# The last two down slabs of a feed-forward stage taken together by output block, and two more buffers for weight halves

## The chip, the cores and the metric

One core of a Trainium2 chip runs the whole kernel. The metric is the time of one execution on the device in microseconds (us); lower is better. Matmuls run on TensorE (PE), vector work on VectorE (DVE), activations and casts on ScalarE (ACT), a few sums on GpSimd (POOL). Transfers are issued from the queues of SyncE (SP) and of ACT.

## The reference, cut to what matters

The input passes through a first block (two layers) and a second block (four layers). A layer of the second block is a mixer (`swa`, `gla`, `fox`, `swa` in turn) and a feed-forward stage, each behind a norm with a learned shift and scale:

```
for i in range(4):
    mod = silu(c) @ ada_w[i] + ada_b[i]
    sh1, sc1, g1, sh2, sc2, g2 = split(mod, 6)
    h = rmsnorm_2(x, norm_gain[i, 0]) * (1 + sc1) + sh1
    x = x + g1 * mixer_i(h)                       # swa, gla, fox, swa
    h = rmsnorm_2(x, norm_gain[i, 1]) * (1 + sc2) + sh2
    g, u = split(h @ w_gu[i], 2)
    x = x + g2 * ((silu(g) * u) @ w_down[i])      # feed-forward
return rmsnorm_2(x, final_norm)
```

There are 256 tokens, 1024 channels and 22 x 128 hidden channels in the feed-forward stage. Everything is float32.

## The kernel before

**Split products.** Each float32 operand is split into a rounded half and the rest (`wh` and `wl` for weights, `gH` and `gL` or `fh` and `fl` for activations), and a product is three matmuls: `wh` by `xH`, `wl` by `xH`, `wh` by `xL` (mm3, L251). In `u_unit` (L397) the same is done for data that isn't normalised yet.

**Weight slabs.** `load_slab` fetches 1 MB of weights into `raw` (three buffers, SP queue) and splits it in two tiles of 1024 columns: ACT casts (`wh`, L161) and DVE subtracts (`wl`, L162). There are four buffers each for `wh` and `wl` (`WB`), so two slabs. In swa layers a tile is split by one instruction, in the other stages by two.

**The feed-forward stage** (`layer2b`) runs over eleven pairs of hidden chunks s = 0 to 10. For each it makes two gate/up units (48 matmuls into a `pm` bank), then silu, a product, and the split into `fh` and `fl`; then the down slab of the pair before (`kacc`) adds 48 matmuls into four accumulator banks `acc`, each of which holds two of the eight output blocks. The last down slab runs by itself: after each bank `x_update` (L969) adds the two finished blocks to the state `xT` on DVE. Per block it also makes the next layer's unnormalised input (`u_feed`: ACT gH L367, DVE gL L368) and the squares for the norm (ACT `sq`, POOL `ssum`).

**Between two stages** the next stage starts with units on the unnormalised input, 48 matmuls each (one in swa layers, two in gla and fox and before each feed-forward stage). In the midst of them come the matmuls that sum the squares (`ms`, L331), and what is left of the units behind the last `ms` covers the chain: ACT `rstd` (Ln L288, Exp L290), then for each of eight channel tiles k a DVE `hn` (L428), an ACT `gH` (L435) and a DVE `gL` (L436). The first unit on normalised data needs tile 0, then 1, and so on.

**The join of the two blocks** is such a place with a double norm (`jn`, `jt`, `jr`: L1016 to L1021; gH L1028, gL L1029). Block 2 opens a pool `cm` with its constants (`band`, `rcos`, `rsin`, `gwa`, `gwg`, `tri`, `causal`, `wf`, `bf`: ten loads from ACT's queue, L896), and the pools of a layer (`zp`, `work`) follow behind `cm` in memory. A pool that reuses memory waits for its last readers. `mi` (L1223) is a first tile of a layer's pool.

**Order.** Each engine works through its instructions in the order that a scheduler fixed when the kernel was built. The numbers `F_AT` and `PADS` shift where tiles lie in memory.

Of the kernel before, what the change touches and what calls it, by code (L numbers as in the profile page):

```python
# [11 lines left out]
F32R = mybir.dt.float32r  # L12
# [41 lines left out]
SCRATCH = 1024  # L54
ROW = 320
SIDE = 32
F_AT = (4, 12, 24)
PADS = (40, 8, 80)
WB = 4
PERM = np.concatenate([np.arange(0, T, 2), np.arange(1, T, 2)])  # L60

# [38 lines left out]
class Kern:  # L100
    def __init__(self, ctx, tc, a):
        self.ctx, self.tc, self.nc, self.a = ctx, tc, tc.nc, a
        nc = self.nc
        self.const = ctx.enter_context(tc.tile_pool(name="const", bufs=1))
        self.slab = ctx.enter_context(tc.tile_pool(name="slab", bufs=1))
        self.act = ctx.enter_context(tc.tile_pool(name="act", bufs=1))
        self.hp = ctx.enter_context(tc.tile_pool(name="hp", bufs=2))
        self.psms = ctx.enter_context(tc.tile_pool(name="psms", bufs=1, space=PSUM))
        self.psum = ctx.enter_context(tc.tile_pool(name="psum", bufs=1, space=PSUM))
        self.ffn, self.nmain = False, 0  # L110
        self.ada = self.ada_stream()
        self.cact = None
        self.rate, self.credit = 0.0, 0.0
        self.ada_done = 0
        self.modc = {}
        self.ms = None
        self.u = None
        self.gates = []
        self.splits = SPLITS
        self.slab_ins = [None] * 8  # L120
        self.fin = None
        self.nuid = 0
        self.load_consts()
        self.const.tile([128, PADS[0]], F32, tag="pad", name="pad0")
        self.hp.tile([128, PADS[1]], F32, tag="pad", name="pad1", bufs=1)

# [38 lines left out]
    def load_slab(self, dram):  # L165
# [12 lines left out]
                next(self.ada, None)  # L178
        return parts

    def split_slab(self, raw):
        parts = []
        for i in range(2):
            H = self.slab.tile([128, 1024], F32R, tag="wh", name=self.uid("wh"), bufs=WB)
            L = self.slab.tile([128, 1024], F32R, tag="wl", name=self.uid("wl"), bufs=WB)
            for q in range(self.splits):
                n = 1024 // self.splits
                c = slice(q * n, (q + 1) * n)
                ins = self.split(raw[:, i * 1024 + q * n:i * 1024 + (q + 1) * n], H[:, c], L[:, c])
                self.slab_ins[i * self.splits + q] = ins  # L190
            parts.append((H, L))
        return parts
# [697 lines left out]
    def block2(self):  # L890
        nc, tc, a = self.nc, self.tc, self.a
        with ExitStack() as ctx:
# [15 lines left out]
            self.fox_bf = cload("bf", [16, 1], a["fox_bf"][0])  # L908
            self.tri = cload("tri", [128, 2, T], a["tri"])
            self.cm.tile([128, PADS[2]], F32, tag="pad", name="pad2")  # L910
            for i in range(DEPTH_2):
                for half in range(2):
                    self.nsq, self.ffn = 3 if (i, half) == (1, 0) else NSQ, half == 1
                    with ExitStack() as lctx:
                        self.zp = lctx.enter_context(tc.tile_pool(name=f"z2_{i}_{half}", bufs=1))
                        self.work = lctx.enter_context(tc.tile_pool(name=f"wk2_{i}_{half}", bufs=2))
                        (self.layer2a if half == 0 else self.layer2b)(i)
# [31 lines left out]
    def acc_banks(self, n=4):  # L949
        return [self.ps("a", "acc") for _ in range(n)]  # L950

    def kacc(self, banks, dram, xs, first, last, after=None):
        parts = self.load_slab(dram)
        for n in range(8):
            for i, (xH, xL) in enumerate(xs):
                H, L = parts[i]
                self.mm3(banks[n // 2][:, (n % 2) * 256:(n % 2) * 256 + 256],
                         H[:, n * 128:(n + 1) * 128], L[:, n * 128:(n + 1) * 128], xH, xL,
                         first and i == 0 and n % 2 == 0, last and i == 1)
            if after and n % 2 == 1:  # L960
                after(n - 1)
                after(n)

    def x_update(self, n, ps, g):
        xv = self.xT[:, n, :]
# [96 lines left out]
    def layer2b(self, i):  # L1062
        nc, a = self.nc, self.a
# [6 lines left out]
        banks = None  # L1070
        pend = []
        nslab = NFF // 2
# [1 line left out]
        def upd(n):  # L1074
            self.x_update(n, banks[n // 2][:, (n % 2) * 256:(n % 2) * 256 + 256], m[:, 40:48])

        def down(s):
            self.kacc(banks, a["w_down"][i, s], pend[s], s == 0, s == nslab - 1,
                      upd if s == nslab - 1 else None)

        for s in range(nslab):
            self.rate = R_FFN if S_ADA <= s < nslab - 1 else 0.0
            xs = []
            for jj in (2 * s, 2 * s + 1):
                t = self.work.tile([128, T], F32, tag="ft", name=self.uid("ft"), bufs=2)
# [8 lines left out]
                else:  # L1094
                    ps = self.unit(a["w_gu"][i, jj], h, "T")
                    last = nc.scalar.activation(t, ps[:, 0:256], AF.Silu)
                    nc.vector.tensor_mul(t, t, ps[:, 256:512])
                f0 = F_AT[s % len(F_AT)]
                H, L = [self.work.tile([128, T + 64], F32R, tag=n, name=self.uid(n), bufs=6)[:, f0:f0 + T]
                        for n in ("fh", "fl")]  # L1100
                self.split(t, H, L)
                xs.append((H, L))
            pend.append(xs)
            if s >= 1:
                if s == 1:
                    banks = self.acc_banks()
                down(s - 1)
            if s == nslab - 1:
                self.preload_ln(last)
        if i + 1 == DEPTH_2:  # L1110
# [1 line left out]
        else:  # L1112
            self.prep_layer(i + 1)
            self.u_begin(self.gp[:, 0:8], self.modc[i + 1][:, 0:8])
        down(nslab - 1)
        if i + 1 == DEPTH_2:
            self.final()

# [524 lines left out]
```

## Time and profile before

| | |
|---|---|
| time, median of 3 runs | 2106.68 us (2104.94 to 2107.19) |
| the profiled execution: its time, its span | 2103.22 us, 2101.3 us |
| PE busy / DVE busy / ACT busy | 2070.5 / 1627.9 / 1203.9 us |
| weight loads by TensorE busy (beside the matmuls) | 2016.7 us |
| mean granted clock of TensorE | 0.998 |
| bytes read by the core | 448 MB, 214 GB/s |

The span is what the trace covers; the time of the run holds 1.92 us more. PE is busy for all but 30.8 us of the span.

### The profile page before, as it was taken

The numbers are of one execution on the slowest core, as the hardware profiler recorded it, in microseconds if no ns is written. First come the engines' busy times: TensorE is split into PE (matmuls) and PEld (weight loads), VectorE is DVE, ScalarE is ACT, GpSimd is POOL, SyncE is SP. The second block draws the span as 40 slices with busy tenths as digits, with TensorE's granted clock in tenths as the row PEclk, the third lists the DMA queues.
The fourth block names the chain that finished last, engine by engine and source line by source line (L and its number), as shares of the span: only waits on it lengthen the run. The fifth ranks groups of instructions, "written<-read, shape, count | busy, mean of one in ns | idle before, by whom it ended". The sixth has DMA issues, their size and how long they took to land.

```text
span 2101.3 us, 42506 instructions
## 1 busy us (share of the span) xinstructions
PE 2070.5 (99%) x17176; PEld 2016.7 (96%) x17176; DVE 1627.9 (77%) x3347; ACT 1203.9 (57%) x2533; POOL 70.7 (3%) x89
## 2 busy tenths in 40 slices
PE   8999999999999999989999999999999999999998
PEld 7999999999999999978999999999989999879998
DVE  7877678997777788797877787877776878868554
ACT  7665555566655554666444666544656544566444
POOL 0000010010000000111000000000000000001000
PEclk9999999999999999999999999999999999999999
DMA  7557668865576578732887432888443888424542
GB/s 265 181 170 257 211 220 292 305 246 191 169 251 221 191 272 316 248 127 90 294 300 279 161 141 101 289 294 284 177 161 121 287 294 309 163 81 170 192 181 101
DMA packets 87830, 452.02 MB, mean 215 GB/s; under 512 B 9978, under 2 KB 19393, under 8 KB 46546
## 3 DMA queue, kind: packets, MB, share of 16 engines
q1 hardware_dynamic: 74736, 438.34, 58.5%
q10 hardware_dynamic: 12898, 10.97, 2.2%
q8 instruction: 134, 2.20, 0.4%
q14 instruction: 62, 0.51, 0.1%
HBM read 448.17 MB, written 1.11 MB: 214 GB/s over the span
## 4 chain that ended last, share of the span: by engine, by line
PE 94%; DVE 4%; ACT 2%; issue 1%; DMA 0%; POOL 0%; DVEq 0%; ACTq 0%
PE pm L251 67%; PE acc L251 11%; PE pa L397 4%; PE pa L251 2%; DVE wl L162 1%; PE po L251 1%; PE ms L331 1%; PE pa L574 1%; PE pa L1134 1%; PE po L1158 1%; ACT s L1143 1%; PE pa L1392 1%; PE pt L1155 0%; PE po L670 0%; PE pa L640 0%
## 5 line engine op out<-in xcount | busy, mean ns | idle before, releaser
L162 DVE TENSOR_TENSOR wl<-raw,wh 128x512 fp32r<-128x512 f32 (+1 forms) x1240 | 832.4, 705 | 276.4 <-ACT wh L161 271.9
L161 ACT CAST wh<-raw 128x512 fp32r<-128x512 f32 (+1 forms) x1240 | 719.2, 632 | 418.3 <-PE pm L251 207.3
L251 PE MATMUL pm<-gH,wh 128*128 128x256 f32 x2112 | 591.4, 281 | 2.1 <-ACT gH L161 2.1
L251 PE MATMUL pm<-gH,wl 128*128 128x256 f32 x2112 | 591.7, 281 | 0.1
L251 PE MATMUL pm<-gL,wh 128*128 128x256 f32 x2112 | 589.6, 281 | 0.1
L251 PEld LDWEIGHTS pm<-gH,wh 128*128 128x128 f32 x2112 | 397.1, 188 | 4.5 <-ACT gH L161 2.8
L251 PEld LDWEIGHTS pm<-gH,wl 128*128 128x128 f32 x2112 | 396.9, 188 | 3.3 <-issue 2.1
L251 PEld LDWEIGHTS pm<-gL,wh 128*128 128x128 f32 x2112 | 395.9, 188 | 3.4 <-issue 2.4
L251 PE MATMUL pm<-hH,wh 128*128 128x256 f32 x1328 | 374.2, 282 | 1.0 <-DVE mrg L162 0.7
L251 PE MATMUL pm<-hL,wh 128*128 128x256 f32 x1328 | 372.8, 281 | 0.8 <-DVE hL L162 0.8
L251 PE MATMUL pm<-hH,wl 128*128 128x256 f32 x1328 | 372.3, 280 | 0.0
L205 DVE CUSTOM_DVE_ANT_0 araw<-araw,cact,pv 128x1024 f32<-128x1024 f32 x192 | 244.3, 1281 | 20.1 <-DMA araw<-ada 19.8
L251 PEld LDWEIGHTS pm<-hH,wh 128*128 128x128 f32 x1328 | 249.7, 188 | 3.6 <-ACT hH L161 1.4
L251 PEld LDWEIGHTS pm<-hL,wh 128*128 128x128 f32 x1328 | 249.7, 188 | 1.4 <-DVE hL L162 1.2
L251 PEld LDWEIGHTS pm<-hH,wl 128*128 128x128 f32 x1328 | 249.7, 188 | 0.5
L251 PE MATMUL acc<-fh,wl 128*128 128x256 f32 x704 | 196.0, 281 | 0.0
L251 PE MATMUL acc<-fh,wh 128*128 128x256 f32 x704 | 194.2, 280 | 0.0
L251 PE MATMUL acc<-fl,wh 128*128 128x256 f32 x704 | 192.5, 281 | 0.0
L251 PEld LDWEIGHTS acc<-fh,wl 128*128 128x128 f32 x704 | 132.2, 188 | 0.0
L251 PEld LDWEIGHTS acc<-fh,wh 128*128 128x128 f32 x704 | 131.6, 188 | 0.0
L251 PEld LDWEIGHTS acc<-fl,wh 128*128 128x128 f32 x704 | 130.4, 188 | 0.0
L251 PE MATMUL pm<-wh,gH 128*128 128x256 f32 x352 | 100.0, 286 | 6.0 <-DVE rt L1175 2.7
(356 smaller groups left out, 3246.1 us busy)
## 6 DMA issues: line engine op xcount, KB each, us to landing
raw<-w_in SPq DMA_DIRECT2D x104, 1024.0 KB, 5.0
araw<-ada SPq DMA_DIRECT2D x192, 512.0 KB, 4.7
raw<-w_gu SPq DMA_DIRECT2D x88, 1024.0 KB, 5.6
raw<-w_down SPq DMA_DIRECT2D x44, 1024.0 KB, 6.1
raw<-swa_w SPq DMA_DIRECT2D x12, 1024.0 KB, 4.7
raw<-gla_w SPq DMA_DIRECT2D x12, 1024.0 KB, 5.4
raw<-fox_w SPq DMA_DIRECT2D x12, 1024.0 KB, 4.8
raw<-w_mem_kv SPq DMA_DIRECT2D x8, 1024.0 KB, 4.8
```

Of the source, the lines that this page charges most:

```text
L161: i1 = self.nc.scalar.copy(H, src)
L162: i2 = self.nc.vector.tensor_sub(L, src, H.bitcast(F32))
L205: nc.vector.tensor_tensor_reduce(out=raw, in0=raw, in1=self.cact, scale=1.0, scalar=self.pv[:, col:col + 1], op0=ALU.mult, op1=ALU.add, ac ...
L251: nc.tensor.matmul(out, l, r, start=start and i == 0, stop=stop and i == 2, skip_group_check=True)
L331: self.nc.tensor.matmul(self.ms[:, col:col + T], self.ones[1024], v, start=first, stop=i == len(self.ms_pend) - 1, skip_group_check=True)
L397: self.nc.tensor.matmul(banks[n][:, 0:nu if i < 2 else T], w[:, c], x, start=kt == 0 and i == 0, stop=kt == NKT - 1 and i == 2, skip_group ...
L574: self.nc.tensor.matmul(S[e][c][:, m * 256:(m + 1) * 256], q, k, start=qi == 0 and ki == 0, stop=ki == 1, skip_group_check=True)
L1134: nc.tensor.matmul(S[e][:, 128 * c:128 + 256 * c], q[r0:r0 + 64, 128 * c:128 * c + 128], k[r0:r0 + 64, 0:128 + 128 * c], start=True, stop= ...
L1143: nc.scalar.activation(s[:, cols], s[:, cols], AF.Exp, scale=-1.0, bias=nm[:, c:c + 1], accum_out=den[:, c:c + 1])
L1158: nc.tensor.matmul(O[r0:r0 + 64, o0:o0 + 256], v(0), pt[:, 0:256], start=True, stop=False, skip_group_check=True)
L1392: nc.tensor.matmul(S[:, hh * 128:(hh + 1) * 128], X[:, c0:c0 + 128], Y[:, c0:c0 + 128], start=True, stop=True)
```

## The change

The tenth and eleventh down slab (s = 9 and 10) of each feed-forward stage are worked through together at the end, in the order of blocks: first the banks 0 and 1 of slab 9, then the banks 0 and 1 of slab 10 with their updates, then bank 2 of both with its update, then bank 3 of both. The ring of `wh` and `wl` tiles grows from four to six in block 2; the two new ones lie in `cm` (16 KB per partition), so that block 2's layer tiles lie 16512 bytes further on. The number of matmuls, casts and subtractions stays. `F_AT` and `PADS` are moved along.

```
-F_AT = (4, 12, 24)
+F_AT = (36, 44, 56)
+XB = 2
-PADS = (40, 8, 80)
+PADS = (40, 8, 112)
 WB = 4
...
+    def wtile(self, tag):
+        ext = self.cm is not None and self.nw % (WB + XB) >= WB
+        pool, t, n = (self.cm, "x" + tag, XB) if ext else (self.slab, tag, WB)
+        return pool.tile([128, 1024], F32R, tag=t, name=self.uid(tag), bufs=n)
...
-            H = self.slab.tile([128, 1024], F32R, tag="wh", name=self.uid("wh"), bufs=WB)
-            L = self.slab.tile([128, 1024], F32R, tag="wl", name=self.uid("wl"), bufs=WB)
+            H, L = self.wtile("wh"), self.wtile("wl")
+            self.nw += 1
...
+    def kacc_block(self, banks, parts, xs, n, first, last):
+        for i, (xH, xL) in enumerate(xs):
+            H, L = parts[i]
+            self.mm3(banks[n // 2][:, (n % 2) * 256:(n % 2) * 256 + 256],
+                     H[:, n * 128:(n + 1) * 128], L[:, n * 128:(n + 1) * 128], xH, xL,
+                     first and i == 0, last and i == 1)
+
+    def kacc_last(self, banks, drams, xs, after):
+        parts = [self.load_slab(d) for d in drams]
+        for s, pair in ((0, 0), (0, 1), (1, 0), (1, 1), (0, 2), (1, 2), (0, 3), (1, 3)):
+            for n in (2 * pair, 2 * pair + 1):
+                self.kacc_block(banks, parts[s], xs[s], n, False, s == 1)
+            if s == 1:
+                after(2 * pair)
+                after(2 * pair + 1)
...
-            if s >= 1:
-                if s == 1:
-                    banks = self.acc_banks()
-                down(s - 1)
+            if s == 1:
+                banks = self.acc_banks()
+            if 1 <= s < nslab - 1:
+                self.kacc(banks, a["w_down"][i, s - 1], pend[s - 1], s == 1)
...
-        down(nslab - 1)
+        self.kacc_last(banks, [a["w_down"][i, s] for s in (nslab - 2, nslab - 1)], pend[-2:], upd)
```

The rows below are pieces of the instruction order. A row gives the line, the operation, what is written and read, and in square brackets the kinds of work that it waits for; lines of the change stand a few higher (L896 is L903, L1223 is L1236, L161 is L163, L428 is L435).

**ACT at the join of the blocks, before.** `wh` are casts, `mi` is the first load into a layer pool of block 2, `jn`, `jt` and `jr` belong to the double norm, `gH` is written tile by tile:

```order
L161 CAST wh1765_11838<-raw1762_11832 128x1024 [waits PE_49]
L1223 DMA mi_12130<-gla_masks 128x768 [waits DMAHW6_49,PE_49,Pool_49]
L1017 ACTIVATE jn_11790<-jn_11790,eps2_83 128x256 [waits DVE_49]
L1018 ACTIVATE jt_11789<-jn_11790 128x256 [waits Activation_49]
L1019 ACTIVATE jn_11790<-jt_11789 128x2x128 [waits Activation_49]
L1021 COPY jr_11788<-ms1707_11428 128x256
L1028 ACTIVATE gH1751_11797<-hn1753_11799,modc0_1689 128x2x128 [waits DVE_49]
L288 ACTIVATE jr_11788<-jr_11788,eps_81 128x256 [waits Activation_49]
L1028 ACTIVATE gH1751_11797<-hn1754_11803,modc0_1689 128x2x128 [waits DVE_49]
L290 ACTIVATE jr_11788<-jr_11788 128x256 [waits Activation_49]
L1028 ACTIVATE gH1751_11797<-hn1755_11807,modc0_1689 128x2x128 [waits DVE_49]
```

Three `gH` follow each other here with two short steps of `jr` between them. The same place in the change, up to the last load ahead of the first `gH`:

```order
L903 DMA band_11694<-mask_swa 128x384 [waits DMAHW4_49,PE_49,Pool_49]
L903 DMA rcos_11696<-rope_cos 128x128 [waits DMAHW6_49]
L903 DMA rsin_11698<-rope_sin 128x128
L903 DMA gwa_11700<-gla_wa 128x128
L1034 ACTIVATE jn_11790<-jn_11790,eps2_83 128x256 [waits DVE_49]
L903 DMA gwg_11702<-gla_wg 17x512
L903 DMA tri16_11704<-tri16 128x128 [waits DMAHW2_49]
L1035 ACTIVATE jt_11789<-jn_11790 128x256 [waits Activation_49]
L903 DMA causal_11707<-mask_fox 128x384
L1036 ACTIVATE jn_11790<-jt_11789 128x2x128 [waits Activation_49]
L1038 COPY jr_11788<-ms1707_11428 128x256
L903 DMA wf_11709<-fox_wf 128x128 [waits DMAHW4_49]
```

The first load into `cm` now stands where `mi` stood, with the same kinds of waits, and eight of the ten loads are ahead of the first `gH`. (Before, all ten stand some 40 rows higher, L896, among the casts of block 1's last layer.) The last of these, `wf`, waits for the semaphore that `band`'s landing raises (DMAHW4). The rows go on:

```order
L1045 ACTIVATE gH1751_11797<-hn1753_11799,modc0_1689 128x2x128 [waits DVE_49]
L903 DMA bf_11711<-fox_bf 16x1 [waits DMAHW5_49]
L1045 ACTIVATE gH1751_11797<-hn1754_11803,modc0_1689 128x2x128 [waits DVE_49]
L903 DMA tri_11713<-tri 128x512 [waits DMAHW6_49]
L295 ACTIVATE jr_11788<-jr_11788,eps_81 128x256 [waits Activation_49]
L163 CAST wh1814_12072<-raw1811_12066 128x1024 [waits PE_49]
L1236 DMA mi_12130<-gla_masks 128x768 [waits DMAHW7_49]
L297 ACTIVATE jr_11788<-jr_11788 128x256 [waits Activation_49]
L163 CAST swh2305_15514<-gwa_11700 128x128 [waits DMAHW0_49]
L1045 ACTIVATE gH1751_11797<-hn1755_11807,modc0_1689 128x2x128 [waits DVE_49]
L1045 ACTIVATE gH1751_11797<-hn1756_11811,modc0_1689 128x2x128 [waits DVE_49]
```

`bf` and `tri` are loads too, and a cast of block 2's weights (`wh1814`) and one of `gwa` now stand between the second and the third `gH`.

**DVE from the third feed-forward stage into the last swa layer, before.** `xT` are the updates, `wl` the subtractions of weights, `hn` starts the normalised tiles:

```order
L162 TENSOR_TENSOR wl3381_23301<-raw3379_23298,wh3380_23300 128x1024
L969 SCALAR_TENSOR_TENSOR xT_74<-acc3110_21183,modc2_11292,xT_74 128x256 x2
L162 TENSOR_TENSOR wl3383_23305<-raw3379_23298,wh3382_23304 128x1024
L969 SCALAR_TENSOR_TENSOR xT_74<-acc3111_21184,modc2_11292,xT_74 128x256 x2
L368 SCALAR_TENSOR_TENSOR gL3361_23175<-xT_74,gp3_23171,gH3360_23174 128x256 x2
L969 SCALAR_TENSOR_TENSOR xT_74<-acc3112_21185,modc2_11292,xT_74 128x256 x2
L368 SCALAR_TENSOR_TENSOR gL3361_23175<-xT_74,gp3_23171,gH3360_23174 128x256
L969 SCALAR_TENSOR_TENSOR xT_74<-acc3113_21186,modc2_11292,xT_74 128x256 x2
L368 SCALAR_TENSOR_TENSOR gL3361_23175<-xT_74,gp3_23171,gH3360_23174 128x256 x5
L162 TENSOR_TENSOR wl3398_23400<-raw3396_23397,wh3397_23399 128x1024
L162 TENSOR_TENSOR wl3400_23404<-raw3396_23397,wh3399_23403 128x1024
L428 SCALAR_TENSOR_TENSOR hn3387_23364<-xT_74,gp3_23171,rstd3384_23359 128x256
```

The same place in the change:

```order
L986 SCALAR_TENSOR_TENSOR xT_74<-acc3110_21183,modc2_11292,xT_74 128x256 x2
L986 SCALAR_TENSOR_TENSOR xT_74<-acc3111_21184,modc2_11292,xT_74 128x256 x2
L375 SCALAR_TENSOR_TENSOR gL3356_23113<-xT_74,gp3_23109,gH3355_23112 128x256
L986 SCALAR_TENSOR_TENSOR xT_74<-acc3112_21185,modc2_11292,xT_74 128x256 x2
L375 SCALAR_TENSOR_TENSOR gL3356_23113<-xT_74,gp3_23109,gH3355_23112 128x256 x3
L986 SCALAR_TENSOR_TENSOR xT_74<-acc3113_21186,modc2_11292,xT_74 128x256 x2
L375 SCALAR_TENSOR_TENSOR gL3356_23113<-xT_74,gp3_23109,gH3355_23112 128x256 x4
L164 TENSOR_TENSOR wl3398_23400<-raw3396_23397,wh3397_23399 128x1024
L164 TENSOR_TENSOR wl3400_23404<-raw3396_23397,wh3399_23403 128x1024
L164 TENSOR_TENSOR wl3439_23608<-raw3437_23605,wh3438_23607 128x1024
L164 TENSOR_TENSOR wl3441_23612<-raw3437_23605,wh3440_23611 128x1024
L435 SCALAR_TENSOR_TENSOR hn3387_23364<-xT_74,gp3_23109,rstd3384_23359 128x256
```

The two `wl` (3381, 3383) that stood ahead of and among the updates have gone ahead of the place, and two more (3439, 3441) stand between the last `gL` and the first `hn`.

**ACT at the entry of the third feed-forward stage, before.** `rstd` twice, then the tiles `gH`; `ft` is the silu of the first hidden chunk:

```order
L288 ACTIVATE rstd3069_20978<-ms3026_20601,eps_81 128x256 [waits PE_49]
L290 ACTIVATE rstd3069_20978<-rstd3069_20978 128x256 [waits Activation_49]
L435 ACTIVATE gH3070_20981<-hn3072_20983,modc2_11292 128x256 [waits DVE_49]
L435 ACTIVATE gH3070_20981<-hn3073_20987,modc2_11292 128x256 [waits DVE_49]
L1092 ACT_TABLE_LOAD
L1092 ACTIVATE ft3080_21015<-ft3080_21015,ub3082_21019 128x256 [waits DVE_49]
L435 ACTIVATE gH3070_20981<-hn3074_20991,modc2_11292 128x256 [waits DVE_49]
L435 ACTIVATE gH3070_20981<-hn3075_20995,modc2_11292 128x256 [waits DVE_49]
L435 ACTIVATE gH3070_20981<-hn3076_20999,modc2_11292 128x256 [waits DVE_49]
```

The same place in the change:

```order
L297 ACTIVATE rstd3069_20978<-rstd3069_20978 128x256 [waits Activation_49]
L163 CAST wh3105_21122<-raw3102_21114 128x512 [waits PE_49]
L163 CAST wh3105_21122<-raw3102_21114 128x512
L442 ACTIVATE gH3070_20981<-hn3072_20983,modc2_11292 128x256 [waits DVE_49]
L442 ACTIVATE gH3070_20981<-hn3073_20987,modc2_11292 128x256 [waits DVE_49]
L163 CAST wh3115_21189<-raw3114_21187 128x512 [waits DMAHW1_49,PE_49]
L163 CAST wh3115_21189<-raw3114_21187 128x512
L1105 ACT_TABLE_LOAD
L1105 ACTIVATE ft3080_21015<-ft3080_21015,ub3082_21019 128x256 [waits DVE_49]
L163 CAST wh3117_21195<-raw3114_21187 128x512 [waits PE_49]
L163 CAST wh3117_21195<-raw3114_21187 128x512
L442 ACTIVATE gH3070_20981<-hn3074_20991,modc2_11292 128x256 [waits DVE_49]
```

Six half casts (3105, 3115, 3117) now stand ahead of the third `gH`; before, they stand behind the fifth.

## Rows read from the trace of the kernel before

**Rows 1.** The profile page: engines' busy time; shares of the chain that ended last.

```profile
PE 2070.5 (99%) x17176; PEld 2016.7 (96%) x17176; DVE 1627.9 (77%) x3347; ACT 1203.9 (57%) x2533; POOL 70.7 (3%) x89
...
PE 94%; DVE 4%; ACT 2%; issue 1%; DMA 0%; POOL 0%; DVEq 0%; ACTq 0%
```

**Rows 2.** Who waited for whom, TensorE: total us, times, longest us.

```profile
PE pa L1134 <- ACT zT L1187: 3.5, 4, 1.5
PE pm L251 <- DVE rt L1175: 2.7, 3, 1.5
PE pm L251 <- ACT gH L435: 2.1, 3, 1.2
PE pm L251 <- ACT gH L161: 2.1, 3, 0.7
PE pa L397 <- DVE gL L368: 0.7, 1, 0.7
```

**Rows 3.** Timeline of DVE, 1797 to 1815: start, us, instructions, idle before, releaser.

```profile
1801.25 1.22 DVE L162 TENSOR_TENSOR wl<-raw,wh 128x1024 fp32r<-128x1024 f32 x1
...
1805.84 0.86 DVE L969 SCALAR_TENSOR_TENSOR xT<-acc,modc,xT 128x256 f32<-128x256 f32 x2
...
1809.10 2.35 DVE L162 TENSOR_TENSOR wl<-raw,wh 128x1024 fp32r<-128x1024 f32 x2
```

**Rows 4.** Timeline of ACT, same place.

```profile
1811.45 0.47 ACT L288 ACTIVATE rstd<-ms,eps 128x256 f32<-128x256 f32 x1 [1.70 <-PE ms L331]
...
1812.98 0.91 ACT L435 ACTIVATE gH<-hn,modc 128x256 fp32r<-128x256 f32 x2 [0.61 <-DVE hn L428]
```

**Rows 5.** Timeline of PE, same place.

```profile
1813.54 0.39 PE L251 MATMUL pm<-wh,gH 128*128 128x256 f32 x1 [1.25 <-ACT gH L435]
```

**Rows 6.** Timeline of ACT at the join of the blocks (ACTq: its queue issues).

```profile
888.92 0.33 ACTq L1223 DMA_DIRECT2D mi<-gla_masks  x1
...
891.44 0.52 ACT L1028 ACTIVATE gH<-hn,modc 128x256 fp32r<-128x256 f32 x1
...
893.04 0.52 ACT L1028 ACTIVATE gH<-hn,modc 128x256 fp32r<-128x256 f32 x1
...
894.38 1.98 ACT L161 CAST wh<-raw 128x1024 fp32r<-128x1024 f32 x2
```

**Rows 7.** Timeline of PE at the join of the blocks.

```profile
892.01 0.38 PE L251 MATMUL pm<-wh,gH 128*128 128x256 f32 x1 [1.17 <-ACT gH L1028]
```

**Rows 8.** Timeline of ACT, 850 to 866: the loads of `cm`.

```profile
854.26 0.35 ACTq L896 DMA_DIRECT2D band<-mask_swa  x1
...
861.69 0.33 ACTq L896 DMA_DIRECT2D wf<-fox_wf  x1
```

**Rows 9.** DMA issues: KB each, median us from issue to landing.

```profile
mi<-gla_masks ACTq DMA_DIRECT2D x1, 384.0 KB, 5.6
band<-mask_swa ACTq DMA_DIRECT2D x1, 192.0 KB, 7.4
causal<-mask_fox ACTq DMA_DIRECT2D x1, 192.0 KB, 3.1
```

**Rows 10.** Windows: stretch, us, PE, PEld, DVE, ACT, POOL busy; PEclk, DMA share, GB/s.

```profile
1850.00:1854.97 4.97, 2.67 (x22) 1.81 (x22) 4.97 (x21) 2.88 (x9) 0.00 (x0) 1.00 0.16 43
1854.97:1858.38 3.41, 3.30 (x12) 1.99 (x12) 3.31 (x18) 1.81 (x7) 0.00 (x0) 0.50 0.59 245
```

**Rows 11.** Timeline of ACT at the entry of the third feed-forward stage.

```profile
1617.78 1.14 ACT L161 CAST wh<-raw 128x512 fp32r<-128x512 f32 x2
1620.00 0.48 ACT L288 ACTIVATE rstd<-ms,eps 128x256 f32<-128x256 f32 x1 [1.09 <-PE ms L331]
...
1622.41 1.28 ACT L1092 ACT_TABLE_LOAD   x1
```

**Rows 12.** Timeline of PE, same place.

```profile
1626.76 0.28 PE L397 MATMUL pa<-gL,wh 128*128 128x256 f32 x1
...
1627.94 0.28 PE L251 MATMUL pm<-gH,wh 128*128 128x256 f32 x1
```

More of the change, by code (lines that the diff above doesn't have):

```diff
@@ L120, in __init__ @@
         self.slab_ins = [None] * 8
+        self.cm, self.nw = None, 0
         self.fin = None
@@ L910, in block2 @@
             self.cm.tile([128, PADS[2]], F32, tag="pad", name="pad2")
+            self.nw = 0
             for i in range(DEPTH_2):
@@ L950, in acc_banks, with kacc @@
         return [self.ps("a", "acc") for _ in range(n)]
-    def kacc(self, banks, dram, xs, first, last, after=None):
+    def kacc(self, banks, dram, xs, first):
         parts = self.load_slab(dram)
         for n in range(8):
[L955 to L962, printed above, removed]
+            self.kacc_block(banks, parts, xs, n, first and n % 2 == 0, False)
+    def kacc_block(self, banks, parts, xs, n, first, last):
[12 more added lines that the diff above has]
+                after(2 * pair + 1)
     def x_update(self, n, ps, g):
@@ L1075, in upd @@
             self.x_update(n, banks[n // 2][:, (n % 2) * 256:(n % 2) * 256 + 256], m[:, 40:48])
-        def down(s):
-            self.kacc(banks, a["w_down"][i, s], pend[s], s == 0, s == nslab - 1,
-                      upd if s == nslab - 1 else None)
         for s in range(nslab):
```

## The prediction, made before the change was run

> **What bounds the kernel now.** The profile page comes first: TensorE is busy for 2070.5 of the 2101.3 us of the span and holds 94% of the chain that ended last [rows 1]. The reader is to see that neither the transfers nor the 1627.9 us of DVE are the bound as a whole. The change takes out no matmul and adds none, so it can only work on the 30.8 us in which TensorE isn't busy, and on the clock. The second view is the list of who waited for whom on TensorE [rows 2]: long entries belong to the attention of the swa layers (`rt`, `zT`: 2.7 and 3.5 us in all), to the tails of attention (`gH` of L161, three waits of 0.7) and to entries of stages (`gH` of L435, 2.1, and `gL` of L368, 0.7). The third view is the timeline at each place that the order of instructions shows as changed: the join of the blocks, the end of the third feed-forward stage, the entry of that stage.
>
> Only one of the four feed-forward ends costs TensorE much: at the third, the 0.7 for `gL` of L368 and the 2.1 for `gH` of L435, of which 1.25 is a single wait [rows 5]. At the entry of the same stage, 7.94 us lie between the start of `rstd` and the first unit on normalised data, and TensorE has no gap there [rows 11, 12]. So what the change means to speed up, the end of the feed-forward stage, is covered nearly everywhere already.
>
> **The order by blocks.** One would expect the updates of six of the eight blocks to come some 24 matmuls earlier. The order doesn't show it, since the scheduler mixes the down matmuls with the last gate/up units and with the first units of the next layer. Counted in TensorE's rows from the first matmul of the last two slabs, the four banks are complete after 63, 72, 84 and 96 matmuls before; in the change after 63, 70, 77, 96 in the first stage, 66, 73, 80, 96 in the third, and 50, 57, 72, 100 in the last. A matmul takes 0.118 us (ten in 1.18 us, first and last shown in [rows 12]), so the third bank comes 0.5 to 0.8 us earlier in the first and third stage, and the last bank, on which the norm hangs, doesn't move. What does get better is DVE at the third end: the last two updates start at 1805.84 because two subtractions of 1.2 us, one of them at 1801.25, sit among the updates [rows 3], and in the change they are ahead. That takes away the wait of 0.7. At the end of the kernel the last bank stays last: -0.2 us (0 to -0.5).
>
> **The new buffers at the join of the blocks.** This is the largest term. The tiles `xwh` and `xwl` make the pool `cm` so large that it lies on tiles that block 1 still reads. The first load of `cm` then has to wait as `mi` does now. `mi` is issued at 888.92 [rows 6]; I take that for `band`. In the trace, `wf` is issued 7.43 us after `band`, just when it has landed [rows 8, 9]: the wait for a landing exists already, but 30 us ahead of the join, where nothing hangs on it. In the change it stands ahead of the first `gH`. How long does `band` take to land there? `causal`, of the same size, took 3.1, `band` 7.4, and `mi`, at this very place but with twice the bytes, 5.6 [rows 9]. I take 4.6, between `causal` and `mi`: landing at 893.5, issue of `wf` 0.33, first `gH` at 893.85 instead of 891.44 [rows 6], 2.4 us late. Up to the third `gH` ACT then has two `gH` (0.9), two steps of `jr` (0.9), a cast of 1.0 (half of the pair of 1.98 in [rows 6]) and the small cast of `gwa` (0.3): 896.95 instead of 893.04, 3.9 late. Behind it on ACT wait the other `gH`, and for these DVE's `gL` and TensorE, which now waits 1.17 for the first [rows 7] and little after it. I take 0.6 off for what slack there is: **+3.3 us**. With 3.1 for the landing it is +1.8, with 7.4 it is +6.1.
>
> A rule of the Trainium skill ("DMA: Bandwidth & Descriptors", section on queues, rings and completion order) speaks for the lower end: each DMA engine goes round between the queues that have work, a packet at a time, so a small load on ACT's queue needn't wait for a large one on SP's. By it I would take the 3.1 of `causal`, and the sum below would be 1.5 us lower. The 7.4 us of `band` in this trace don't agree with it as a promise.
>
> **The entry of the last swa layer.** Two more subtractions (1.2 each, [rows 3]) and one more cast come ahead of the first `hn`. The second cast writes a buffer that the unnormalised unit frees with its last matmul, and that unit now has only 2 matmuls left behind the last `ms` (8 before). So after Ln (0.5) come the cast (1.0), the subtraction (1.2), `hn` (0.45), `gH` (0.5): the first tile is there 3.65 us after the start of Ln, against 2.04 now (1811.45 to 1813.49, half of the pair in [rows 4]). TensorE waits 1.25 + 1.6 + 0.7 for the six matmuls less of cover = 3.55 us in one piece; the 0.7 for `gL` and the other 0.85 for `gH` go, because the splits that now stand between the later tiles are done. 3.55 - 2.8 = **+0.8 us** (-1 where the splits are done earlier than I think, +2 where the later waits stay).
>
> **The entry of the third feed-forward stage.** Behind the last `ms` are now 44 matmuls of cover, before 69: the first normalised unit comes 25 x 0.118 = 2.95 us sooner, 5.0 us after the start of `rstd`, and wants the third tile 0.7 us later, at 5.7. ACT has ahead of the third `gH`: Ln and Exp (0.9), three pairs of half casts (1.14 each, [rows 11]), two `gH` (0.9), the table load (1.28), the silu (0.45) and `gH` itself (0.5): 7.45. **+1.7 us** (0 to 3). The first and last feed-forward stage have the same 44, but less on ACT; gla and fox lose six matmuls of cover (0.7): together **+0.5** (0 to 2).
>
> **What the buffers bring.** In the swa, gla and fox layers the last unit of the output projection moves ahead into the attention, a piece of 48 matmuls (5.6 us) that can stand in for waits. The places that it reaches are the tails: the three waits of 0.7 for `gH` of L161 and part of those for `zT` [rows 2]. I take two of the three: **-1.5 us** (0 to -2.6). The `rt` and `zT` waits in mid-attention have no such unit beside them in the order.
>
> **The clock.** Once in block 2 the granted clock falls to half, for 3.41 us, behind a stretch in which TensorE was busy for 2.67 of 4.97 us [rows 10]. Where I forecast waits of some 3.5 us in one piece (the join, the last swa entry), it may fall too. A stretch like that costs at most 1.7 us (half of 3.41); I take half of one: **+0.8** (0 to 3.4).
>
> **The sum.** 3.3 + 0.8 + 1.7 + 0.5 + 0.8 - 1.5 - 0.2 = +5.4 us on the profiled execution's 2103.22, 2108.6. The median of the runs is 3.46 above the profiled execution; the same step put on it gives 2106.68 + 5.4 = 2112.1 us, +0.26%. A difference of under 0.2% (4.2 us) is about what a measurement of this kernel can't tell from none.
>
> **The rivals.**
> (a) The deeper ring pays in the swa layers. ACT and DVE have a slab split ahead when the attention begins, and the units that this readies fill all of TensorE's waits for `rt`, `zT` and `gH` of L161 (8.3 us, [rows 2]), and the entry of the last swa layer's 2.8 go, since the splits are behind it. With the join and the clock as above that is -8.3 - 2.8 + 4.1 = -7.0: 2099.7 us. For it: those waits are TensorE's largest. Against it: in the order only one unit moves in each layer, and the waits in mid-attention stay without one. It decides from the point at which a unit's `wl` is ready ahead of the first wait for `rt`.
> (b) The loads of `cm` don't hold up the join: the tiles that they lie on are free earlier than I read, or `band` lands at once. Without the join and the clock the sum is +1.3: 2108.0. For it: 3.1 us for `causal`. Against it: `band` has the same kinds of waits as `mi`, which waited to 888.92.
> (c) The change does nothing: the banks are complete where they were, and the entries' casts find slack: 2106.7. For it: three of four feed-forward ends have no wait to lose. Against it: the join.
>
> **Chances.** That the join is held: 0.58, of which 0.14 with a sum under 4.2 us; (a) 0.22; (b) 0.14; (c) 0.06. Faster by over 0.2% (under 2102.5): 0.22; within: 0.14 + 0.14 + 0.06 = 0.34; slower (over 2110.9): 0.44. The likeliest is 2112 us; with the bounds of the landing and of the entries its own range is 2107 to 2118. The range for all goes down into (a): 2101 to 2117.
>
> **What would show it.** The join: `band` issued near 889, `wf` at its landing, the first `gH` after 893, and TensorE's wait there of over 3 us instead of 1.17. The last swa entry: one wait of about 3.5 us for `gH` of L435, no wait for `gL` of L368. The third feed-forward entry: a wait for the third tile. The tails: fewer of the 0.7 waits. The clock: half speed behind the join. I am wrong if the loads of `cm` are issued well ahead of 888, if the waits of the swa attentions shrink by more than 3 us, or if the down matmuls' pace changes with the tiles' places in memory, which the order can't tell.

## The result, and the profile after

The change runs in 2128.93 us (median of 4, 2126.02 to 2134.30) against 2105.81 (2104.86 to 2107.19): a ratio of 1.0114, 95% interval 1.0101 to 1.0126. It is slower by 23 us, over 4 times the +5.4 that was forecast, and outside the range. The profiled execution took 2128.64 us with a span of 2126.8.

The page of the profile after, to set beside [rows 1]:

```profile
PE 2079.1 (98%) x17176; PEld 2026.1 (95%) x17176; DVE 1626.0 (76%) x3347; ACT 1202.2 (57%) x2533; POOL 65.6 (3%) x89
...
PE 90%; DVE 5%; ACT 3%; DMA 1%; issue 1%; POOL 0%; DVEq 0%; ACTq 0%; SPq 0%; POOLq 0%
```

The span grew by 25.5 us. TensorE's time without work went from 30.8 to 47.7 (span less busy), +16.9; the other 8.6 are busy time that got longer, with the same 17176 matmul records. The list of who waited for whom on TensorE, to set beside [rows 2]:

```profile
PE pm L258 <- ACT wh L163: 7.3, 2, 3.7
...
PE pm L258 <- ACT gH L442: 5.7, 3, 3.5
PE pm L258 <- ACT gH L1045: 5.3, 2, 4.2
...
PE pm L258 <- DVE wl L164: 3.0, 4, 2.0
...
PE pa L290 <- ACT gH L442: 1.9, 2, 1.2
PE pm L258 <- DVE rt L1188: 1.9, 2, 1.5
```

The first and the fourth line are new to the list: TensorE waits for weights, `wh` and `wl`. The three waits of 0.7 for `gH` of L161 and the 0.7 for `gL` of L368 are gone; the forecast had two of the three, and the `gL`.

**The join** went as forecast. The timeline of ACT there, to set beside [rows 6]:

```profile
888.20 0.34 ACTq L903 DMA_DIRECT2D band<-mask_swa  x1
...
893.36 0.33 ACTq L903 DMA_DIRECT2D wf<-fox_wf  x1
893.74 0.52 ACT L1045 ACTIVATE gH<-hn,modc 128x256 fp32r<-128x256 f32 x1 [1.45 <-DMA band<-mask_swa]
```

`band` is issued at 888.20, `wf` 5.16 us later, when it has landed, and the first `gH` follows at 893.74. TensorE waits 4.19 and 1.08 us for tiles there, against 1.17 and two times 0.25 before.

**The first feed-forward entry** is where the forecast was blind. Timelines of ACT and of TensorE:

```profile
986.36 1.02 ACT L314 ACTIVATE sq<-xT 128x256 f32<-128x256 f32 x3
991.68 0.47 ACT L295 ACTIVATE rstd<-ms,eps 128x256 f32<-128x256 f32 x1 [4.30 <-issue]
...
994.03 1.13 ACT L163 CAST wh<-raw 128x512 fp32r<-128x512 f32 x2
995.18 1.28 ACT L1105 ACT_TABLE_LOAD   x1
...
997.69 1.12 ACT L163 CAST wh<-raw 128x512 fp32r<-128x512 f32 x2
999.44 0.51 ACT L442 ACTIVATE gH<-hn,modc 128x256 fp32r<-128x256 f32 x1 [0.63 <-DVE hn L435]
999.86 4.24 ACT L163 CAST wh<-raw 128x512 fp32r<-128x512 f32 x8
```

```profile
984.00 0.28 PE L404 MATMUL pa<-gH,wh 128*128 128x258 f32 x1
...
990.14 0.59 PE L338 MATMUL ms<-ssum,ones 128*128 128x256 f32 x2
990.57 1.03 PE L338 MATMUL ms<-sq,ones 128*128 128x256 f32 x4
...
1000.51 0.58 PE L258 MATMUL pm<-gH,wh 128*128 128x256 f32 x1 [3.73 <-ACT wh L163]
```

Read them together. ACT has the last squares done at 987.4 (986.36 + 1.02) and then nothing to do for 4.30 us, although `rstd` is next: the `ms` matmuls that it needs stand in TensorE's order behind some 51 matmuls of the unnormalised units (984.00 to 990.14). (The sum on POOL that they also need is done at 987.8.) From `rstd` at 991.68 the cover lasts only 5.1 us. The weights of the first normalised unit are cast at 999.86, because that split is held behind the fifth `gH` (999.44). TensorE waits 3.73 us for them. Before, that entry had 70 matmuls behind the last `ms` and no wait. The last feed-forward entry does the same (3.60), the third waits 1.75 for `gH`.

The same entry in the kernel before, on ACT and on TensorE:

```profile
985.08 0.47 ACT L288 ACTIVATE rstd<-ms,eps 128x256 f32<-128x256 f32 x1 [0.93 <-PE ms L331]
...
991.52 3.21 ACT L161 CAST wh<-raw 128x512 fp32r<-128x512 f32 x6
```

```profile
984.38 0.60 PE L331 MATMUL ms<-sq,ones 128*128 128x256 f32 x2
...
993.07 0.28 PE L251 MATMUL pm<-gH,wh 128*128 128x256 f32 x1
```

From the start of `rstd` to that cast were 6.4 us, and 8.0 to the first normalised unit. In the change the cast comes after 8.2 us and the cover ends after 5.1. So two things came together: 2.9 us less cover, and a chain that is 1.7 us longer, with two pairs of casts for later slabs among its tiles (994.03 and 997.69).

**Inside the second feed-forward stage** TensorE waits once for a split on DVE. Timelines of DVE and of TensorE:

```profile
1334.37 1.28 DVE L212 CUSTOM_DVE_ANT_0 araw<-araw,cact,pv 128x1024 f32<-128x1024 f32 x1
...
1335.58 1.28 DVE L212 CUSTOM_DVE_ANT_0 araw<-araw,cact,pv 128x1024 f32<-128x1024 f32 x1
...
1337.38 0.68 DVE L164 TENSOR_TENSOR wl<-raw,wh 128x512 fp32r<-128x512 f32 x1
```

```profile
1338.12 0.39 PE L258 MATMUL pm<-gH,wl 128*128 128x256 f32 x1 [2.03 <-DVE wl L164]
```

Two reductions of the stream that makes the modulation (`araw`, L212, 1.28 us each) stand in DVE's order ahead of the `wl` that TensorE wants.

**The clock.** Windows of the trace, with the granted clock behind the five busy times:

```profile
893.09:903.33 10.24, 7.80 (x32) 7.19 (x33) 8.91 (x16) 7.81 (x14) 1.10 (x1) 0.50 0.62 212
998.91:1005.73 6.82, 4.77 (x20) 4.48 (x21) 6.82 (x15) 5.47 (x11) 0.00 (x0) 0.50 0.57 184
1196.88:1200.29 3.41, 3.21 (x14) 2.75 (x15) 3.41 (x7) 3.41 (x8) 0.00 (x0) 0.50 0.88 300
1647.44:1650.85 3.41, 3.41 (x18) 3.41 (x18) 3.21 (x7) 3.28 (x8) 0.00 (x0) 0.50 0.65 269
1835.17:1842.00 6.83, 6.42 (x30) 6.11 (x29) 6.65 (x13) 5.23 (x9) 0.00 (x0) 0.50 0.42 154
1937.57:1944.40 6.83, 5.42 (x23) 5.13 (x24) 6.83 (x13) 5.44 (x11) 0.00 (x0) 0.50 0.66 220
sum 37.54, PE 31.03 PEld 29.08 DVE 35.83 ACT 30.64 POOL 1.10; mean PE 5.17 PEld 4.85 DVE 5.97 ACT 5.11 POOL 0.18
```

In these six stretches of mid-kernel the clock is at half (0.50, 1.2 GHz), in the other parts at full speed. Each begins within a single wait of TensorE or up to 2 us behind its end; these waits last 1.2 to 4.2 us. Not each such wait has one: behind the 2.03 us that end at 1338.12 the clock stays full. From 1835.17 to 1842.00 TensorE is busy for 6.42 us with 30 matmuls, where full speed makes 54 (0.118 each). Before, there was one such stretch in mid-kernel, with 3.30 us busy [rows 10]. Half of the 31.0 us busy at half speed, less half of the 3.3 before, is some 14 us: an estimate of what the clock adds to the busy time. The busy time grew by only 8.6, so outside these stretches it is some 5 us shorter than before, which no run here takes apart.

### The profile page after: what moved, and what is told of

It reads as the page before. It is cut to its first block, busy times and chain, and to the rows that moved or that the text cites. A ratio compares the mean times of both kernels' runs of the same rounds, so it can differ in the third digit from the quotient of the medians.

```text
span 2126.8 us, 42550 instructions
## 1 busy us (share of the span) xinstructions
PE 2079.1 (98%) x17176; PEld 2026.1 (95%) x17176; DVE 1626.0 (76%) x3347; ACT 1202.2 (57%) x2533; POOL 65.6 (3%) x89
## 4 chain that ended last, share of the span: by engine, by line
PE 90%; DVE 5%; ACT 3%; DMA 1%; issue 1%; POOL 0%; DVEq 0%; ACTq 0%; SPq 0%; POOLq 0%
PE pm L258 67%; PE acc L258 12%; DVE wl L164 2%; PE pa L258 2%; PE pa L404 1%; PE po L258 1%; PE pa L581 1%; PE pa L1147 1%; PE po L1171 1%; ACT s L1156 1%; DVE hn L435 1%; ACT wh L163 1%; PE pa L1405 1%; PE ms L338 0%; DVE gL L443 0%
## 5 line engine op out<-in xcount | busy, mean ns | idle before, releaser
L163 ACT CAST wh<-raw 128x512 fp32r<-128x512 f32 (+1 forms) x1240 | 719.2, 632 | 412.1 <-PE pm L258 208.9
L212 DVE CUSTOM_DVE_ANT_0 araw<-araw,cact,pv 128x1024 f32<-128x1024 f32 x192 | 244.4, 1281 | 26.2 <-DMA araw<-ada 25.9
```

The lines of the kernel that those rows point to most:

```text
L163: i1 = self.nc.scalar.copy(H, src)
L212: nc.vector.tensor_tensor_reduce(out=raw, in0=raw, in1=self.cact, scale=1.0, scalar=self.pv[:, col:col + 1], op0=ALU.mult, op1=ALU.add, ac ...
```

## The experiments

Ratios are to the kernel before, run beside each on the same chip.

**Which half of the change.** Buffers alone (the old `kacc` and `down` put back), the order by blocks alone, and the change's memory layout alone:

```
e1_bufs:    def down(s): self.kacc(banks, a["w_down"][i, s], pend[s], s == 0, s == nslab - 1, ...)   # as before
e2_blocks: -XB = 2          +XB = 0             (and F_AT, PADS as before)
e3_layout: +for t in ("xwh", "xwl"):
           +    for n in range(2):
           +        self.cm.tile([128, 1024], F32R, tag=t, name=f"{t}_{n}", bufs=2)   # in the kernel before, unused
```

> Six buffers with the old order of the down slabs (each slab by itself). Theory: the buffers alone make the loss, since with them the order of instructions at the entries of the stages is that of the change (52 and 44 matmuls ahead of and behind the last ms at the first, third and last feed-forward entry). Then 2126 to 2131 us, with the waits of TensorE for wh at two feed-forward entries (3.7 and 3.6) still there. Rival 1, the order by blocks is what costs: near 2106. Rival 2, the places of the tiles in memory slow the matmuls: as the change, 2126 to 2131, so this run doesn't tell it from the theory.

> The order by blocks alone, with four buffers and tiles where they were before. Theory: nothing is lost, three of four feed-forward ends had no wait to lose, and the third may gain the 2.8 us of waits at most: 2102 to 2107. Rival 1 (the order by blocks costs): 2115 and more. Rival 2 (places in memory): 2104 to 2107 too.

> The kernel before with the change's places in memory: the four new tiles lie in cm, unused; four buffers and the old order of the slabs; the ten loads of cm stand in the join's chain as in the change, and the other entries' orders are those of before. Theory (the order at the entries makes the loss): only the join pays, 3 to 5 us with the clock behind it: 2109 to 2112. Rival 2 (the places in memory slow the matmuls): 2114 and more, with TensorE's busy time up over the whole of block 2. Rival 3 (the join's delay is taken up later): 2106.

Buffers alone: 2132.94, 1.0129 (1.0113 to 1.0144), no better than the change; the waits of 3.72 and 3.60 for `wh` stand in its trace. Order by blocks alone: 2111.60, 1.0028 (1.0019 to 1.0036), clearly slower, which neither I nor the theory had. TensorE's waits there:

```profile
PE pa L404 <- DVE wl L164: 6.2, 4, 2.0
...
PE pa L404 <- ACT wh L163: 1.0, 3, 0.6
```

Two slabs held at once fill all four buffers, so the weights of the next layer's first unit come late, by 1.9 to 2.0 us at three ends of feed-forward stages. So the order by blocks wants a third slab. Layout alone: 2105.78, 1.0001 (0.9991 to 1.0010), under what the theory had, and rival 3's number. The places in memory cost nothing that can be measured. And neither do the ten loads, which this kernel issues as late as the change does, although TensorE's waits at the join grow to 1.70 and 2.07 us.

**The join, with the loads early again.** The new tiles in a pool of their own behind `cm`:

```
+            self.xw = ctx.enter_context(tc.tile_pool(name="xw", bufs=1))
-        pool, t, n = (self.cm, "x" + tag, XB) if ext else (self.slab, tag, WB)
+        pool, t, n = (self.xw, "x" + tag, XB) if ext else (self.slab, tag, WB)
```

> The change, but the new tiles lie in a pool of their own behind cm, so that the ten loads of cm are issued early again, as before. Theory: the join gets back its 3.5 us of TensorE's waits and the half clock behind it (892 to 904), 6 to 9 us in all: 2120 to 2123; the other five stretches at half clock stay. Rival 2 (places in memory slow the matmuls everywhere): only the waits come back, 2125 to 2126. Rival 3, the join's delay is taken up by later slack: 2127 to 2130.

2129.58, 1.0111 (1.0098 to 1.0125): nothing came back that these runs can tell. ACT's timeline at the join shows why:

```profile
889.91 0.33 ACTq L1237 DMA_DIRECT2D mi<-gla_masks  x1
891.87 1.04 ACT L163 CAST wh<-raw 128x1024 fp32r<-128x1024 f32 x1 [2.72 <-PE pa L404]
892.82 0.50 ACT L1035 ACTIVATE jn<-jn,eps 128x256 f32<-128x256 f32 x1
...
894.93 0.91 ACT L1046 ACTIVATE gH<-hn,modc 128x256 fp32r<-128x256 f32 x2
```

With the loads out of the way, a cast for a slab further on, which has to wait 2.72 us for a buffer that TensorE's unnormalised unit frees, stands ahead of the double norm's first step on ACT and holds it up, by 1.25 us: its input is ready on DVE at 891.57. On DVE three subtractions of weights (from 887.29, 3.50 us) stand ahead of that input too. TensorE waits 3.66 us for the first tile instead of 4.19. The loads and the splits put ahead are two things, each of which alone makes over 3.6 us of waits here. Since the wait stayed, this run doesn't tell what the join is worth.

**The hold of the first normalised split** (`if k == gk: self.gates.append(...)`), behind the second tile instead of the fifth:

```
-GKF = 4
+GKF = 1
```

> The change with GKF 1 instead of 4: the split of the first normalised gate/up unit's weights is held behind the second tile gH instead of the fifth. Theory: at the first and last feed-forward entry TensorE waits for that split because it is held behind the fifth gH and the cover behind the last ms is 44 matmuls; with GKF 1 the waits of 3.7 and 3.6 for wh fall to under 1.5 each (for a gH instead), and the half clock behind them shortens: 5 to 9 us less than the change, 2120 to 2124. Rival 4, the cover alone decides and the hold doesn't matter: the same waits stand at gH, 2127 to 2131.

2130.42, 1.0114 (1.0100 to 1.0128), rival 4. At the first entry the 3.73 and 0.45 became 1.49 for `wl` and 1.65 for `gH`, at the third the wait grew to 3.13. The wait for `wh` went, as the theory had it, but others came: with 44 matmuls of cover something of the chain is late, whichever it is.

**Where the deeper ring hurts.** Each with the pool behind `cm`:

```
e6_ffn:  ext = self.xw is not None and self.ffn and self.nw % (WB + XB) >= WB
e7_mix:  ext = self.xw is not None and not self.ffn and self.nw % (WB + XB) >= WB
e9_down: ext = self.ext        # True only while kacc_last loads drams[0]
```

> The change with the new tiles in a pool behind cm and used in the feed-forward stages only; the mixers keep to four. The order shows 26 and 70 matmuls around the last ms at the first and last feed-forward entry again. Theory: the mixers' deeper ring is what pulls the output projection's last unit ahead and takes the cover; the waits of 3.7 and 3.6 for wh go with their half clocks, as does the join's; gla and the last swa layer keep their entries: 2110 to 2116. Rival 5, the splits put ahead by the ring in the feed-forward stages cost most: 2120 and more.

> The mirror of the one above: the new tiles used in the mixers only. The order shows 52 and 44 matmuls at the first, third and last feed-forward entry. Theory: the three feed-forward entries still wait (3 to 4 us each, with half clock behind): 2118 to 2127. Rival 5: 2106 to 2113.

> The order by blocks, with the new tiles (in a pool behind cm) used for the tenth down slab alone, so that the two slabs are held at once and every other slab keeps to four buffers. Order by blocks with four buffers made TensorE wait 1.9 to 2.0 us for wl at three feed-forward ends. Theory: these waits go and nothing is pulled ahead in the mixers: 2103 to 2107; at the third feed-forward end the 2.8 of before may shrink. Rival 1 (the order by blocks itself costs): 2110 to 2113 as with four buffers.

Feed-forward stages only: 2119.64, 1.0065 (1.0051 to 1.0078), more than I allowed and close to rival 5's 2120. The waits for `wh` at the entries are gone there, as expected; three waits of 1.6 to 2.0 for `wl` inside the stages stand in the trace. Mixers only: 2126.90, 1.0098 (1.0084 to 1.0112), of which some 6 are the order by blocks with four buffers, if the two add up. At the three feed-forward entries TensorE waits 2.07, 1.95 and 1.85 us for `wh`, not 3 to 4, and the clock stays full there. So the ring costs in both places: in the mixers it takes the cover, and the chain from `rstd` to the cast at the first entry is 6.5 us again, as before; in the feed-forward stages it puts splits ahead. The tenth down slab only: 2103.97, 0.9992 (0.9983 to 1.0001): the whole loss is gone, and what the change does to the down slabs, given its third slab and nothing else, is worth nothing that these runs can tell from zero.

**The unit that is pulled ahead.** With the ring in the mixers, the last unit of the output projection goes ahead of the third one on TensorE. It has a bank for each of its two blocks, so it used to end with one update 1.45 us ahead of the other; the third unit, which now comes last, shares one bank and gives both updates at its end (984.20 in the trace after). The squares come later against TensorE's stream, and `ms` goes behind the first unnormalised unit. Held back:

```
-                ps = self.unit2(w[j], o)
+                with self.tc.issue_after(self.mm.ins):      # self.mm: the matmul traced last
+                    ps = self.unit2(w[j], o)
e12_holdgate, besides:
-                    self.gates.append((i1.ins, i2.ins))
+                    self.gates += [(i1.ins, i2.ins)] * 3
```

> The run with the new tiles in the mixers only, with the same hold. Against that run's 2127 theory A expects the three waits for wh at the feed-forward entries (2.1, 1.9, 1.9) and their half clocks to go: 2116 to 2121; the waits of 2.0 for wl at two feed-forward ends, which four buffers make with the order by blocks, stay. Rival 5: 2124 to 2128.

> The change, with the last unit of each output projection held on TensorE behind the third one, as it stood before; six buffers everywhere. The order shows 25 and 71 matmuls around the last ms at all four feed-forward entries. Theory A (the unit that the deeper ring pulls ahead takes the cover of the next entry): the waits at the first, third and last feed-forward entry, 4.2 + 2.0 + 4.0 us, go with the half clock behind them, and the tails' waits of 0.7 come back: 2113 to 2119. Rival 5 (the splits that the ring puts ahead of the norms' chains make the loss, whatever the cover): the waits stay, 2123 and more.

> The hold, and behind each norm the splits of the next three slabs (not of one) are kept behind the same tile gH, so that no split of a later slab stands ahead of a norm's chain; six buffers everywhere, the loads of cm still late. Theories A and B together (the pulled unit, and the splits ahead of the chains) make up the loss: 2104 to 2111. If 2114 or more is left, a third cause is open (the modulation's reductions on DVE, or the late loads).

In the mixers-only kernel the hold does what theory A says: 2118.27, 1.0053 (1.0038 to 1.0068), and the waits for `wh` are gone. In the whole change it brings 2125.55, 1.0089 (1.0074 to 1.0104), where theory A had 2113 to 2119: the interval touches that of the change (1.0101 to 1.0126), so a gain there is hardly shown. Its trace has no wait for `wh` at the entries either; what it has is this:

```profile
PE pm L258 <- DVE wl L164: 6.7, 6, 2.0
...
PE pm L258 <- ACT gH L1046: 5.3, 2, 4.2
PE pm L258 <- ACT gH L442: 4.3, 3, 3.5
...
PE pm L258 <- ACT gH L163: 2.1, 3, 0.7
```

The waits at the join (L1046) and at the last swa entry (L442) are those of the change, and the tails' waits of 0.7 (L163) are back. The 6.7 us for `wl` hold three waits of 1.6, 2.0 and 2.0, each inside a feed-forward stage, behind reductions of `araw` as above; in the change itself there was one of them. Holding back three slabs' splits is no way out: 2129.06, 1.0114 (1.0097 to 1.0131); now the splits of the hidden chunks (`fl`, 2.65 in one piece; `fh`, 2.2) and later tiles are late, and the waits at the join are 1.71, 2.10 and 2.15.

**The modulation's stream.**

```
-R_FFN = 1.25
+R_FFN = 1.43
-S_ADA = 2
+S_ADA = 3
```

> The change with the hold and with the modulation's stream started at s = 3 instead of 2 in each feed-forward stage, 1.43 per slab instead of 1.25. Theory C (the two reductions ahead of a split that TensorE waits for are the third part of the loss): the waits of 1.6, 2.0 and 2.0 for wl go: 2116 to 2120 against the hold's 2125.6. Rival 6 (DVE is full there, and another late split takes the place): the waits move, 2123 to 2127.

> The new tiles in the feed-forward stages only, with the same later start of the stream. Against that run's 2119.6, theory C: the waits of 1.6, 2.0 and 2.0 for wl go, with the half clock at 1328 to 1336: 2111 to 2115. Rival 6: 2117 to 2121.

> Control: the kernel before with the same later start of the stream. It has no such waits, so nothing is to be won: 2104 to 2108. If it is faster by 3 or more, the start of the stream matters by itself and the two runs beside it say less.

With the hold: 2115.92, 1.0045 (1.0030 to 1.0060), 9.6 less. In the feed-forward-only kernel: 2110.98, 1.0020 (1.0011 to 1.0030), 8.7 less. In the kernel before: 2106.01, 0.9994 (0.9985 to 1.0004), nothing. The waits for `wl` of 1.6 to 2.0 are in neither trace. Theory C is shown for these two kernels; the later stream alone, in the change itself, was not run.

**What is left, and the version that the runs point to.** `e16_all` adds the pool behind `cm` to `e13_holdada`, and two held slabs in the mixers; `e17_downada` is `e9_down` with the later stream.

> The run with the hold and the later stream, and besides: the new tiles in a pool behind cm (the loads early again), and in the mixers the splits of two slabs, not one, kept behind the norm's chain. Theory B (what stands ahead of the chains makes the rest): TensorE's wait at the join falls from 5.3 to under 2.5, at the last swa entry from 4.1 to under 3: 2107 to 2112 against 2115.9. Rival 7 (the ring costs by itself): 2114 to 2118.

> The order by blocks with the new tiles for the tenth down slab alone, and the later start of the modulation's stream. The run without the later start was at 0.9992 of before, the control with it alone at 0.9994: if both hold and add, 0.9986, 2102 to 2105; if neither is real, 2105 to 2108.

2117.10, 1.0050 (1.0035 to 1.0064): no gain. TensorE's wait at the join did fall (1.17, 0.26 and 0.83) and the first one at the last swa entry too (1.95), but a wait of 2.55 for a later tile came in there, since the held splits now stand between the tiles. The number is rival 7's, and the trace shows again a wait that moved. And 2105.57, 0.9994 (0.9986 to 1.0003): the later stream adds nothing to `e9_down`; no version here beats the kernel before by more than the runs can tell.

## Why the prediction was wrong

The sign and the kind of cause were right: the buffers, through the order at the joins of stages, not the order by blocks. The size was not. By its terms:

| term | forecast | TensorE's waits, before to after |
|---|---|---|
| join of the blocks | +3.3 | 1.7 to 5.3: +3.6 |
| last swa entry | +0.8 | 3.4 to 3.9: +0.6 |
| third feed-forward entry | +1.7 | 0 to 2.0 |
| first and last feed-forward, gla, fox entries | +0.5 | 0 to 4.2, 4.0, 2.1, 0.8: +11 |
| inside the second feed-forward stage | none | 0 to 2.0 |
| tails of the attentions | -1.5 | three of 0.7 gone: -2.1 |
| clock | +0.8 | busy time +8.6; busy at half speed 3.3 to 31.0 |

**The step that failed** is the sentence "The first and last feed-forward stage have the same 44, but less on ACT; gla and fox lose six matmuls of cover (0.7): together +0.5 (0 to 2)". I followed the tiles `gH` to the first unit, and not its weights. Their split is held behind the fifth `gH`, so the chain from `rstd` is not 7.4 us, as I had it at the third entry, but 8.7 (991.68 to the end of the first half cast, 1000.4), and it is the same at the last entry; against 5.1 us of cover that gives 3.6, and the trace shows 3.73 and 3.60. The four places together, booked at +0.5, made 11 us of waits. `GKF = 1` then showed that the hold isn't the cause in itself: without it other waits stand there. The cover is the larger part, 2.9 of the 4.6 us that the entry lost, and the casts put ahead by the ring are the rest. I also took the 2.95 us less cover as a given of the order, without asking what had put `ms` behind the unit. The runs with the hold name it: the output projection's last unit, which I had booked as a gain (the tails, -1.5) and which did bring that gain. In time this is shown in the mixers-only kernel (1.0098 to 1.0053); in the whole change the hold took the waits for `wh` away too, and most of the loss stayed (1.0114 to 1.0089).

**The second failure** is the clock. Half of one half-speed stretch was taken for two places; there were six stretches, each beside a wait. By the busy time they made a third of the loss (8.6 of 25.5); by the estimate from their rows they added some 14 us, part of which the rest of the kernel made up.

**Left out altogether** was DVE inside the feed-forward stages. The change of order that I looked at ended with the entries; the two `araw` ahead of a `wl` cost 8.7 and 9.6 us where they were tested, waits and clock together, with three such waits in each kernel. In the change there is one, of 2.03 us, and its price there was not measured.

**The largest term was right in the trace, and the time does not show it.** Layout alone has the late loads and TensorE's waits of 3.8 us at the join, and runs in 2105.8. And with the loads early the change is no faster, but there the wait at the join stayed at 3.66. Whether the 3.6 us more at the join carry through to the end in the change itself was not told apart.

**The order by blocks** was booked as -0.2 with six buffers, and `e9_down` agrees with it within its interval. That the order costs some 6 us with four buffers was no part of the forecast.

**Open** stays about 10 us: with the hold, the later stream, the loads early and splits held in the mixers, 1.0050 is left. Every splitting of a slab that is taken away from one chain turns up in front of another, and no run here shows one single owner of the rest. The parts don't add up either: the ring in the feed-forward stages costs 0.65%, in the mixers 0.98% (with the 0.28% of the blocks), together 1.14%.

## What to carry to other kernels

A deeper ring of buffers on engines that work in a fixed order wasn't free prefetch here (1.0129 by itself): work that may run ahead is put ahead of other work, and where a chain without slack follows, that chain waits. With the extra buffers given to the one place that holds more at once (here the tenth down slab), the loss was gone. When an order moves at one entry of a stage, follow all that the first unit behind it needs, its weights too, and do so at every entry of that form.

## What the hardware showed that I had not expected

Half-clock stretches follow waits that look harmless: behind the 1.25 us that end at 1196.21 the clock is at half from 1196.88 to 1200.29, and in the run with the order by blocks alone the join, whose waits were nearly those of before (1.17, 0.25, 0.47), had half clock behind it, where the kernel before, in its profiled execution, had none. Its windows there:

```profile
892.00:896.00 4.00, 3.13 (x13) 2.18 (x12) 3.86 (x9) 3.60 (x7) 0.82 (x1) 0.73 0.33 134
896.00:900.00 4.00, 4.00 (x21) 4.00 (x20) 4.00 (x7) 2.15 (x4) 0.00 (x0) 0.50 0.24 35
900.00:904.00 4.00, 4.00 (x33) 4.00 (x33) 2.54 (x5) 1.33 (x3) 0.96 (x2) 0.92 0.55 227
```

So nearly the same waits may or may not cost the clock. A small thing beside it: `band`, 192 KB, had landed 5.16 us after its issue at the join, and 7.4 us after it at its old place [rows 9].
